# Attention heads of a two-layer trunk: weights issued one head ahead, a second pair of raw buffers, scratch moved between pools, later steps of a head called earlier

## The chip, the cores and the metric

One core of a Trainium2 chip runs the whole program. The time is device microseconds from start to end of one launch; a median over several runs is compared. TensorE (PE) does the matmuls, VectorE (DVE) and ScalarE (ACT) the element work, SyncE (SP) issues nearly all DMAs, and the engines synchronise by semaphores.

## The reference

```python
def reference(x, ...):                       # x: 1 x 1024 x 1024, float32
    h = x
    for layer in range(2):
        u = rmsnorm(h, norm_mix[layer])
        mix = hgrn2_mixer(u, ...) if layer == 0 else dilated_attention_mixer(u, ...)
        h = h + mix
        h = h + swiglu_ffn(rmsnorm(h, norm_ffn[layer]), ...)
    return rmsnorm(h, final_norm)

def dilated_attention_mixer(u, w_qkv, w_out, cos, sin):
    qkv = (u @ w_qkv).reshape(B, S, 3, 12, 128)
    q, k, v = rope(qkv[:, :, 0]), rope(qkv[:, :, 1]), qkv[:, :, 2]
    for gi, (window, dilation) in enumerate(((128, 1), (512, 4), (2048, 16))):   # 4 heads each
        o_g, lse_g = dilated_window_group(q, k, v of the group's heads, window, dilation)
    alpha = softmax over the 3 groups of lse
    return (o * alpha).reshape(B, S, 1536) @ w_out
```

The change lies in the attention mixer of layer 1 alone. The recurrent mixer, both feed-forward layers and the norms stay as they are.

## The kernel before

Everything is float32; a product is made of three single-pass matmuls of a rounded high part and a low part (`halves`: ACT rounds, DVE subtracts). The kernel runs on the Tile framework. The Python text gives each instruction a place in a priority order; when the program is built, a planner with its own estimate of durations fixes the order of each engine's instructions and gives each tile one of the buffers of its tag (`slots`, line 49: "wr" 2, "wx" 2, "wh" 3, "wl" 3, "ws" 4, "va" 16, "vb" 12, "vc" 8, each 128 x 1024 float32). An instruction can be put ahead of earlier text if its inputs and a buffer are there. On the chip each engine then works through its own list strictly in order.

After the values of all heads are made and stored to DRAM (`vd`), the loop over `heads` (line 942) goes through twelve heads in the order (j, gi), head number n = gi * 4 + j, so n = 0, 4, 8, 1, 5, 9, 2, 6, 10, 3, 7, 11. For each head:

- `attn_qk` (line 779) loads the raw weights of q and k (`r_aq`, `r_ak`, 512 KB each, both in "wr"), and `pair` turns them into seven split weights a to g (`pair_weights`, lines 691 to 704, alternating between "wh" and "wl"). Seven products of twelve 512-column matmuls follow (`seeded`, lines 710 to 712): b11, t1, t2, b21, t3, b22, t4, which use the weights a, b, c, d, e, f, g. After every product comes one `tick()`. The partial sums are copied between PSUM banks by ACT (lines 731, 734, 737). `rope` (lines 765 to 777) writes q and k ("vc"), with a scratch tile `sz` ("wx").
- The later steps of a head are put in a calendar by tick: scores in two parts (`s1`, `s2`, lines 829 and 830, with the softmax of line 840 in `s2`), the transposes of the probabilities (`t1`, `t2`, lines 873 and 874) and the product with the values (`values`, lines 883 to 889, with the value tile `avv` in "vc" loaded by `attn_value`). They run in the ticks of the next two heads. The probabilities `ap` lie in "ws": two tiles for a head of group 0 or 1, one for group 2.
- In the group-2 head of j, `attn_merge(j - 1)` (lines 929 to 938) rescales the three outputs of j - 1: six pieces `mg` in "ws", each loaded from `od`, with its weights `dw`, multiplied by DVE (line 937) and stored back.

After the loop the nine merged outputs are loaded (`am`, "vc") and split (`aov0` to `aov8`). `part_out` multiplies them for the first two output blocks d0 and d1 while the last heads' steps still tick. The last three outputs (`late`) are rescaled by `wb`, a broadcast of `dw` that needs all scores of j = 3 (lines 980 to 985), then split as `aov9` to `aov11` and multiplied. `mixer_out` goes on with the other six blocks.

Of the kernel before, what the change touches and what calls it, by code (L numbers as in the profile page):

```python
# [17 lines left out]
D = 1024  # L18
KT = D // P
H = 8  # L20
NH = 12
# [19 lines left out]
def trunk_kernel(ctx, tc, x, cols, consts, w_in, w_hout, w_qkv, w_aout, w_ffn, w_down, out):  # L41
# [9 lines left out]
    def big(tag, name, dt=F32):  # L51
        return gp.tile([P, T], dt, tag=tag, name=name, bufs=slots[tag])
# [4 lines left out]
    def mmps(name):  # L57
        return pmm.tile([P, 512], F32, tag="mm", name=name)
# [4 lines left out]
    def hs(hh):  # L63
        return slice(hh * 512, hh * 512 + 512)

    def cs(c):
        return slice(c * P, c * P + P)


    def load_raw(src, n, name, tag="wr"):  # L70
        raw = big(tag, f"r_{name}")
        nc.sync.dma_start(raw[:, 0:n], src)
        return raw
# [144 lines left out]
    for i0 in range(0, NMASK, 8):  # L218
        n = min(8, NMASK - i0)
# [34 lines left out]
    def hgrn_fq(j):  # L254
        f = scaled(unit(w_in[H + j], v, f"f{j}"), "vc", f"f{j}")
        nc.scalar.activation(f[:], f[:], AF.Sigmoid)
        nc.vector.tensor_scalar(f[:], f[:], omlb[:, j:j + 1], lb[:, j:j + 1], ALU.mult, ALU.add)
        kk = big("vc", f"kk{j}")
        nc.vector.tensor_scalar(kk[:], f[:], -1.0, 1.0, ALU.mult, ALU.add)
        return f, kk, gated(j, 0, "q")  # L260
# [160 lines left out]
    for j in range(H):  # L421
        f, kk, q = hgrn_fq(j)
# [151 lines left out]
    def mixer_out(l, spill, load, vs, parts, name, begun={}):  # L574
        nrm = Norm(name)
        h, ops = {}, {}

        def weights(d):
            n = len(vs) // parts * P
            return [load_w((w_hout, w_aout)[l][d][:, i * n:i * n + n], n, f"{name}w{d}_{i}") for i in range(parts)]  # L580

        for d in DORDER:
            t = big("vc", f"{name}h{d}")
            nc.sync.dma_start(t[:], load[d])
            ws = () if d in begun else weights(d)
            if d == KT - 1:
                w_head[l] = ffn_w_head(l, 0)
            ps = begun.get(d) or [mmps(f"p_{name}{d}_{hh}") for hh in range(2)]
            m = len(vs) // parts
            for i, (whi, wlo) in enumerate(ws):  # L590
                mm3(ps, whi, wlo, 0, vs[i * m:i * m + m], first=(i == 0), last=(i == parts - 1))
            h[d] = add_res(ps, t, d, nrm, spill, 2 * l + 1, name)
            if d >= 4:
                ops[d - 4] = ffn_operands(d - 4, h[d - 4], h[d], op_tags[l][7 * (d - 4):7 * (d - 3)], name)
        return ops, nrm

    ops, nm = mixer_out(0, hd[0], x, ov, 1, "n1")
# [5 lines left out]
    qops = [{n: big("va", f"q{n}_{kk}", F32R) for n in ("b12", "b11")} for kk in range(4)]  # L603
# [83 lines left out]
    def w_half(src, name):  # L687
        wn[0] += 1
        return halves(big(("wh", "wl")[wn[0] % 2], name, F32R), src)

    def pair_weights(ga, up, name):
        g0, g1, u0, u1 = ga[:, hs(0)], ga[:, hs(1)], up[:, hs(0)], up[:, hs(1)]
        w = {"b11": w_half(g0, f"{name}a")}
        nc.vector.tensor_sub(g0, g0, u0)
        nc.vector.tensor_add(u0, u0, u1)
        w["t1"] = w_half(u0, f"{name}b")
        nc.vector.tensor_sub(u0, u1, g0)
        w["t2"] = w_half(u0, f"{name}c")
        w["b21"] = w_half(g1, f"{name}d")
        nc.vector.tensor_sub(g1, g1, u0)  # L700
        w["t3"] = w_half(g0, f"{name}e")
        w["b22"] = w_half(g1, f"{name}f")
        w["t4"] = w_half(u1, f"{name}g")
        return w

    def seeded(ps, w, ops, n, onto=True):
        for kk in range(4):
            wh, wl = w[n][:, cs(kk)], w[n][:, 512 + kk * P:512 + kk * P + P]
            bh, bl = ops[kk][n][:, 0:512], ops[kk][n][:, 512:T]
            nc.tensor.matmul(ps[:], wh, bh, start=(kk == 0 and not onto), stop=False, skip_group_check=onto)  # L710
            nc.tensor.matmul(ps[:], wh, bl, start=False, stop=False, skip_group_check=onto)
            nc.tensor.matmul(ps[:], wl, bh, start=False, stop=(kk == 3), skip_group_check=onto)
# [4 lines left out]
    def later(n, step):  # L717
        steps.setdefault(n, []).append(step)

    def tick():  # L720
        for step in steps.pop(clock[0], ()):
            step()
        clock[0] += 1

    def pair(ga, up, ops, s5, name):
        w = pair_weights(ga, up, name)
        p1, p5, p2, p3 = [mmps(f"{n}_{name}") for n in ("p1", "p5", "p2", "p3")]
        seeded(p1, w, ops, "b11", False)  # L730
        nc.scalar.copy(p2[:], p1[:])
        tick()
        seeded(p5, w, ops, "t1", False)
        nc.scalar.copy(s5, p5[:])
        tick()
        seeded(p2, w, ops, "t2")
        nc.scalar.copy(p3[:], p2[:])
        tick()
        seeded(p1, w, ops, "b21")
        yield p1  # L740
        tick()
        seeded(p3, w, ops, "t3")
        yield p3
        tick()
        seeded(p2, w, ops, "b22")
        yield p2
        tick()
        seeded(p3, w, ops, "t4")
        yield p3
        tick()  # L750
# [25 lines left out]
            nc.vector.tensor_mul(tv, src[:], cb[:, hs(hh)])  # L776
        nc.vector.tensor_add(tv, tv, z)

    def attn_qk(j, gi):
        n = gi * 4 + j  # L780
        ga = load_raw(w_qkv[n], D, f"aq{n}")
        up = load_raw(w_qkv[NH + n], D, f"ak{n}")
        sz = big("wx", f"sz{n}")
        s5, z = sz[:, 0:512], sz[:, 512:T]
        p = pair(ga, up, qops, s5, f"a{n}")
        q = big("vc", f"aq{n}")
        k = big("vc", f"ak{n}")
        rope(q, next(p), None, 0, z)
        rope(k, next(p), s5, 1, z)
        rope(q, next(p), s5, 1, z)  # L790
        rope(k, next(p), None, 0, z)
        for _ in p:
            pass
        return q, k
# [49 lines left out]
    def attn_value(j, gi):  # L844
        n = gi * 4 + j
        vv = big("vc", f"avv{n}")
        src = vd[:, cs(n)]
        if gi == 0:
            nc.sync.dma_start(vv.rearrange("p (c m) -> p c m", m=P), src.rearrange("(c p) m -> p c m", p=P))
        elif gi == 1:  # L850
            sv = src.rearrange("(i p r) m -> p r i m", p=P, r=4)
            for r in range(4):
                nc.sync.dma_start(vv[:, r * 256:r * 256 + 256].rearrange("p (i m) -> p i m", m=P), sv[:, r])
        else:
            nc.sync.dma_start(vv.rearrange("p (c m) -> p c m", m=P), src.rearrange("(p c) m -> p c m", c=8))
        return vv
# [71 lines left out]
    heads = [(j, gi) for j in range(4) for gi in range(3)]  # L928
# [10 lines left out]

    dws = {}  # L940
    sts = [sp.tile([P, 3, 8, 2], F32, tag="st", name=f"st{j}", bufs=2) for j in range(4)]
    for i, (j, gi) in enumerate(heads):
        q, k = attn_qk(j, gi)
        if gi == 2 and j:
            attn_merge(j - 1)
        blocks, ptiles, s1, s2 = attn_scores(j, gi, sts[j], q, k)
        t1, t2, values = attn_out(j, gi, blocks, ptiles)
        vv = {}
        at = clock[0]
        later(at + 2, s1)  # L950
        later(at + 4, s2)
        if gi == 2:
            later(at + 4, lambda j=j: dws.setdefault(j, attn_weights(j, sts[j])))
        later(at + 9, lambda t1=t1, vv=vv, j=j, gi=gi: (vv.setdefault(0, attn_value(j, gi)), t1()))
        later(at + 11, t2)
        later(at + 13, lambda values=values, vv=vv: values(vv[0]))


    ov, begun, aw = [], {}, {}
# [5 lines left out]
    def part_out(d, lo, hi):  # L965
        if d not in begun:
            begun[d] = [mmps(f"p_n3{d}_{hh}") for hh in range(2)]
        i = lo // 6
        if (d, i) not in aw:
            aw[d, i] = load_w(w_aout[d][:, i * 768:i * 768 + 768], 768, f"n3w{d}_{i}")  # L970
        mm3(begun[d], *aw[d, i], (lo - 6 * i) * P, ov[lo:hi], first=(lo == 0), last=(hi == NH))

    d0, d1 = DORDER[:2]
    at = clock[0]
    for upto, d, lo, hi in ((2, d0, 0, 6), (4, d1, 0, 6), (9, d0, 6, 9), (11, d1, 6, 9), (13, None, 0, 0)):
        while clock[0] <= at + upto:
            tick()
        if d is not None:
            part_out(d, lo, hi)
    for gi in range(3):  # L980
        o = late[gi]
        wb = big("wx", f"wb{gi}")
        nc.sync.dma_start(wb[:], dws[3][gi].partition_broadcast(P))
        nc.vector.tensor_mul(o[:], o[:], wb[:])
        ov.append(split(o, "vb", f"aov{9 + gi}"))
# [3 lines left out]
    ops, nm = mixer_out(1, hd[2], hd[1], ov, 2, "n3", begun)  # L989
# [115 lines left out]
```

## Time and profile before

| | |
|---|---|
| median of 3 runs | 2633.09 us (2630.01 to 2633.51) |
| the profiled execution | 2631.86 us, span 2630.1 us |
| TensorE busy | 2538.7 us, 97% of the span |
| VectorE, ScalarE busy | 1739.6 us (66%), 908.0 us (35%) |
| mean granted TensorE clock | 0.987 |

A row of a timeline is start, duration, engine, line, operation, output and inputs, count, and in brackets the idle time of the engine before it with what ended it. A granted clock of 1.00 is TensorE's full 2.4 GHz; 0.5 would be 1.2 GHz throughout.

### The profile page before, as it was taken

How to read it: one execution, taken by the hardware profiler on the slowest of the kernel's cores; microseconds unless marked ns; L12 is line 12 of the kernel's file. 1: busy time of each engine (PE TensorE's matmuls, PEld its weight loads, DVE VectorE, ACT ScalarE, POOL GpSimd, SP SyncE). 2: the span in 40 equal slices, each digit the busy share in tenths (PEclk: the TensorE clock that was granted, in tenths of full speed). 3: DMA queues.
4: the chain of work that ended last, by engine and by line, in shares of the span. 5: the costliest groups of instructions: out<-in, count | busy, mean ns of one | idle time of the engine just before them, and what ended most of it. 6: DMA issues, size and time to landing. Idle time of an engine off the chain costs nothing.

```text
span 2630.1 us, 30557 instructions
## 1 busy us (share of the span) xinstructions
PE 2538.7 (97%) x11804; PEld 2110.8 (80%) x11804; DVE 1739.6 (66%) x3079; ACT 908.0 (35%) x1400; POOL 129.9 (5%) x107
## 2 busy tenths in 40 slices
PE   8999999999999999999999998896999999999998
PEld 6888888778888888888887776775878888887887
DVE  7888888967777776524515665564468777775336
ACT  5222222344232333313423554454343332332212
POOL 1111111111000000000000000000010000000000
PEclk9999999999999999999999998998999999999999
DMA  3111111132222225422232124427422222236323
GB/s 143 33 33 33 33 33 33 49 137 88 88 80 88 80 83 192 159 75 77 81 113 80 49 66 137 135 75 219 137 77 92 85 80 87 74 103 234 107 59 127
DMA packets 113761, 246.78 MB, mean 94 GB/s; under 512 B 23632, under 2 KB 50640, under 8 KB 113616
## 3 DMA queue, kind: packets, MB, share of 16 engines
q1 hardware_dynamic: 113616, 244.83, 28.9%
q8 instruction: 93, 1.52, 0.2%
q14 instruction: 52, 0.43, 0.0%
HBM read 189.07 MB, written 55.72 MB: 93 GB/s over the span
## 4 chain that ended last, share of the span: by engine, by line
PE 77%; DVE 9%; DMA 7%; ACT 4%; issue 2%; POOL 1%; SPq 0%; DVEq 0%; POOLq 0%; ACTq 0%
PE pt L483 6%; PE pt L482 6%; PE pt L481 6%; PE pfw L125 6%; PE pfw L127 6%; PE pfw L124 6%; PE pb L482 4%; PE pb L483 4%; PE pb L481 4%; PE p_n L124 2%; PE p_n L125 2%; PE p_n L127 2%; PE pv L654 2%; PE pv L655 2%; PE pv L656 2%
## 5 line engine op out<-in xcount | busy, mean ns | idle before, releaser
L563 DVE TENSOR_TENSOR h<-pfw,h 128x512 f32<-128x512 f32 (+1 forms) x104 | 63.6, 645 | 197.5 <-PE pfw L127 197.4
L108 ACT CAST h_fw<-r_fw 128x896 fp32r<-128x896 f32 (+1 forms) x60 | 58.2, 973 | 237.6 <-PE pfw L125 216.9
L108 ACT CAST h_fa<-r_fg 128x1024 fp32r<-128x1024 f32 x44 | 46.5, 1056 | 199.7 <-PE pt L482 184.8
L108 ACT CAST h_fb<-s 128x1024 fp32r<-128x1024 f32 x44 | 46.4, 1054 | 171.2 <-PE pb L482 159.6
L829 PE MATMUL as<-ak,aq 128*128 128x256 f32 (+1 forms) x192 | 64.6, 455 | 30.2 <-DVE st L830 22.9
L342 DVE COPY_PREDICATED at<-lm,lv 128x192 f32<-128x192 uint8 (+2 forms) x288 | 82.0, 352 | 4.2 <-PE lv L327 3.3
L829 PEld LDWEIGHTS as<-ak,aq 128*128 128x128 f32 x192 | 46.5, 281 | 42.2 <-DVE st L830 28.1
L156 POOL TENSOR_TENSOR rs_n<-ms_n,half 128x8 f32<-128x8 f32 (+2 forms) x7 | 9.3, 1334 | 1359.0 <-DVE ms_n L154 1359.0
L655 PE MATMUL pv<-vw,qb 128*128 128x512 f32 x192 | 74.8, 390 | 0.0
L654 PE MATMUL pv<-vw,qb 128*128 128x512 f32 x192 | 74.8, 389 | 0.0
L656 PE MATMUL pv<-vw,qb 128*128 128x512 f32 x192 | 74.7, 389 | 0.0
L494 DVE TENSOR_TENSOR s<-r_fu 128x512 f32<-128x512 f32 x44 | 30.3, 691 | 63.5 <-DMA r_fu<-in_w_ffn_dram 63.5
L482 PE MATMUL pb<-n3b,h_fa 128*128 128x512 f32 x176 | 68.7, 390 | 2.6 <-DVE n3b L456 2.6
L109 DVE TENSOR_TENSOR l_fw<-r_fw,h_fw 128x896 fp32r<-128x896 f32 (+1 forms) x60 | 67.0, 1120 | 5.5 <-ACT h_fw L108 4.8
L482 PE MATMUL pb<-n1b,h_fa 128*128 128x512 f32 x176 | 68.6, 390 | 1.2 <-DVE n1b L456 1.2
L481 PE MATMUL pb<-n3b,h_fa 128*128 128x512 f32 x176 | 68.8, 391 | 0.5 <-ACT n3b L455 0.5
L481 PE MATMUL pt<-n3t,h_fb 128*128 128x512 f32 x176 | 68.9, 392 | 0.0
L483 PE MATMUL pt<-n3t,l_fb 128*128 128x512 f32 x176 | 68.7, 390 | 0.0
L482 PE MATMUL pt<-n3t,h_fb 128*128 128x512 f32 x176 | 68.7, 390 | 0.0
L481 PE MATMUL pb<-n1b,h_fa 128*128 128x512 f32 x176 | 68.6, 390 | 0.0
L481 PE MATMUL pt<-n1t,h_fb 128*128 128x512 f32 x176 | 68.6, 390 | 0.0
L483 PE MATMUL pb<-n3b,l_fa 128*128 128x512 f32 x176 | 68.5, 389 | 0.0
(1505 smaller groups left out, 7949.1 us busy)
## 6 DMA issues: line engine op xcount, KB each, us to landing
r_fu<-in_w_ffn_dram SPq DMA_DIRECT2D x44, 512.0 KB, 3.6
r_fg<-in_w_ffn_dram SPq DMA_DIRECT2D x44, 512.0 KB, 3.6
act<-g SPq DMA_DIRECT2D x44, 512.0 KB, 2.6
st<-act SPq DMA_DIRECT2D x44, 512.0 KB, 4.2
r_fw<-in_w_down_dram SPq DMA_DIRECT2D x44, 448.0 KB, 3.4
h<-hd SPq DMA_DIRECT2D x16, 512.0 KB, 5.6
r_fw<-in_w_down_dram SPq DMA_DIRECT2D x16, 512.0 KB, 3.6
vr<-in_w_qkv_dram SPq DMA_DIRECT2D x24, 256.0 KB, 3.2
```

The source lines that it names most:

```text
L108: nc.scalar.copy(hi[:, a:b], src[:, a:b])
L124: nc.tensor.matmul(p[:, 0:b - a], wh, vh[:, a:b], start=(first and i == 0), stop=False)
L125: nc.tensor.matmul(p[:, 0:b - a], wh, vl[:, a:b], start=False, stop=False)
L127: nc.tensor.matmul(p[:, 0:b - a], wl, vh[:, a:b], start=False, stop=(last and i == n - 1))
L342: nc.vector.copy_predicated(av[:, :, d:4, :], mk[:, :, d:4, :], pv[:, :, s0:s0 + 4 - d, :])
L481: nc.tensor.matmul(ps[:], wh, bh, start=(kk == 0), stop=False)
L482: nc.tensor.matmul(ps[:], wh, bl, start=False, stop=False)
L483: nc.tensor.matmul(ps[:], wl, bh, start=False, stop=(kk == 3))
L654: nc.tensor.matmul(ps[:], vh, wh, start=(kb == 0), stop=False)
L655: nc.tensor.matmul(ps[:], vh, wl, start=False, stop=False)
L656: nc.tensor.matmul(ps[:], vl, wh, start=False, stop=(kb == 7))
L829: nc.tensor.matmul(ps[:, o:o + w], tok(q, gi, b * P, P), tok(k, gi, ks[0] * P, w), start=True, stop=True)
```

## The change

A new `qk_weights` issues the loads and the splitting of a head's weights; the loop calls it one head ahead. The raw k weights go to "wx", so that two heads' raw weights can be in memory at once; the scratch `sz` moves from "wx" to "vc". In the calendar `t1` moves from 9 to 8 ticks after the head, `t2` from 11 to 9, `values` from 13 to 10. After the loop the parts of the output product are cut and placed differently between the ticks, and `wb` moves from "wx" to "wr".

```diff
-    def pair(ga, up, ops, s5, name):
-        w = pair_weights(ga, up, name)
+    def pair(w, ops, s5, name):
...
-    def attn_qk(j, gi):
+    def qk_weights(j, gi):
         n = gi * 4 + j
         ga = load_raw(w_qkv[n], D, f"aq{n}")
-        up = load_raw(w_qkv[NH + n], D, f"ak{n}")
-        sz = big("wx", f"sz{n}")
+        up = load_raw(w_qkv[NH + n], D, f"ak{n}", "wx")
+        return pair_weights(ga, up, f"a{n}")
+
+    def attn_qk(j, gi, w):
+        n = gi * 4 + j
+        sz = big("vc", f"sz{n}")
...
+    qw = {heads[0]: qk_weights(*heads[0])}
     for i, (j, gi) in enumerate(heads):
-        q, k = attn_qk(j, gi)
+        if i + 1 < NH:
+            qw[heads[i + 1]] = qk_weights(*heads[i + 1])
+        q, k = attn_qk(j, gi, qw.pop((j, gi)))
...
-        later(at + 9, lambda ...: (vv.setdefault(0, attn_value(j, gi)), t1()))
-        later(at + 11, t2)
-        later(at + 13, lambda ...: values(vv[0]))
+        later(at + 8, lambda ...: (vv.setdefault(0, attn_value(j, gi)), t1()))
+        later(at + 9, t2)
+        later(at + 10, lambda ...: values(vv[0]))
...
-    for upto, d, lo, hi in ((2, d0, 0, 6), (4, d1, 0, 6), (9, d0, 6, 9), (11, d1, 6, 9), (13, None, 0, 0)):
+    for upto, d, lo, hi in ((1, d0, 0, 3), (4, d0, 3, 6), (4, d0, 6, 9), (9, d1, 0, 6), (10, d1, 6, 9)):
         while clock[0] <= at + upto:
             tick()
-        if d is not None:
-            part_out(d, lo, hi)
+        part_out(d, lo, hi)
     for gi in range(3):
         o = late[gi]
-        wb = big("wx", f"wb{gi}")
+        wb = big("wr", f"wb{gi}")
```

## Rows read from the trace of the kernel before

**Rows 1.** The page, part 1: busy time, share of the span, instructions

```profile
PE 2538.7 (97%) x11804; PEld 2110.8 (80%) x11804; DVE 1739.6 (66%) x3079; ACT 908.0 (35%) x1400; POOL 129.9 (5%) x107
```

**Rows 2.** Stretches: bounds, length, busy PE PEld DVE ACT POOL, clock, DMA share, GB/s

```profile
1576.60:1614.00 37.40, 30.01 (x140) 25.61 (x138) 19.08 (x42) 13.79 (x25) 0.00 (x0) 0.86 0.65 183
1775.70:1846.10 70.40, 50.49 (x220) 40.17 (x219) 32.55 (x55) 29.18 (x48) 0.00 (x0) 0.85 0.70 213
1846.10:1944.50 98.40, 98.40 (x436) 81.50 (x435) 46.83 (x63) 34.04 (x51) 8.30 (x6) 1.00 0.34 111
```

**Rows 3.** Waits of TensorE in the loop over heads: total, times, longest

```profile
PE as L829 <- DVE st L830: 22.9, 9, 5.6
...
PE p_a L710 <- ACT p_a L731: 4.6, 3, 2.5
```

**Rows 4.** A wait of TensorE from the loop's end to 1850 us

```profile
PE p_n L124 <- ACT aov0h L144: 4.3, 1, 4.3
```

**Rows 5.** Timeline at head 5, DVE, SP and PE, weights of head 9

```profile
1522.04 0.68 DVE L612 TENSOR_TENSOR a5g<-r_ak,a5g 128x512 fp32r<-128x512 f32 x1
1522.75 0.33 SPq L72 DMA_DIRECT2D r_ak<-in_w_qkv_dram  x1
1526.52 0.69 DVE L694 TENSOR_TENSOR r_aq<-r_aq,r_ak 128x512 f32<-128x512 f32 x1 [1.79 <-DMA r_ak<-in_w_qkv_dram]
1527.86 0.42 DVE L830 CUSTOM_DVE_ANT_0 ap<-as,kon 128x256 f32<-128x256 f32 x1
1528.34 1.13 PE L829 MATMUL as<-ak,aq 128*128 128x256 f32 x4 [2.09 <-DVE st L830]
```

**Rows 6.** Stretches after such waits, columns as in rows 2

```profile
1495.60:1504.60 9.00, 7.17 (x27) 6.06 (x27) 5.25 (x20) 1.72 (x3) 0.00 (x0) 0.81 0.02 9
...
1658.00:1678.50 20.50, 19.43 (x93) 16.68 (x94) 11.91 (x32) 9.82 (x27) 0.00 (x0) 0.92 0.01 1
1750.00:1760.00 10.00, 9.18 (x26) 6.77 (x27) 4.67 (x13) 3.57 (x7) 0.00 (x0) 0.83 0.44 124
```

**Rows 7.** Timeline at the start of head 11, ACT and PE

```profile
1744.79 2.18 ACT L889 COPY ao<-apo 128x512 f32<-128x512 f32 x2
1750.19 0.58 ACT L731 COPY p_a<-p_a 128x512 f32<-128x512 f32 x1
1750.82 0.50 PE L710 MATMUL p_a<-qt,a11c 128*128 128x512 f32 x1 [2.47 <-ACT p_a L731]
```

**Rows 8.** Timeline at the end of the merges, DVE and PE

```profile
1607.31 0.68 DVE L937 TENSOR_TENSOR mg<-mg 128x512 f32<-128x512 f32 x1
1608.26 0.84 PE L829 MATMUL as<-ak,aq 128*128 128x128 f32 x2 [5.58 <-DVE st L830]
1708.56 0.84 PE L829 MATMUL as<-ak,aq 128*128 128x128 f32 x2 [4.95 <-DVE st L830]
```

**Rows 9.** Timeline of the loop's end, PE, SP and DVE

```profile
1772.35 3.51 PE L883 MATMUL apo<-ap,avv 128*128 128x128 f32 x30
1774.55 0.47 SPq L935 DMA_DIRECT2D mg<-od  x1
1806.27 0.28 DVE L830 CUSTOM_DVE_ANT_0 ap<-as,even 128x128 f32<-128x128 f32 x1
1818.76 0.52 SPq L905 DMA_DIRECT2D dn<-st  x1
1835.98 1.65 PE L124 MATMUL p_n<-aov9h,h_n3w 128*128 128x512 f32 x3 [10.23 <-ACT aov9h L144]
```

**Rows 10.** Instructions of line 710: durations in ns, first and last start

```profile
L710 PE MATMUL p_a<-qt,a0b x4: 389/389/389, 1410.7 to 1412.7; 128*128 128x512 f32 x4
...
L710 PE MATMUL p_a<-qt,a0e x4: 389/389/389, 1418.8 to 1420.9; 128*128 128x512 f32 x4
```

**Rows 11.** DMA issues, 1400 to 1850 us: count, KB each, median us to landing

```profile
r_ak<-in_w_qkv_dram SPq DMA_DIRECT2D x11, 512.0 KB, 5.0
avv<-vd SPq DMA_DIRECT2D x8, 512.0 KB, 6.1
```

More of the change, by code (lines that the diff above doesn't have):

```diff
@@ L777, in rope @@
         nc.vector.tensor_add(tv, tv, z)
-    def attn_qk(j, gi):
+    def qk_weights(j, gi):
         n = gi * 4 + j
         ga = load_raw(w_qkv[n], D, f"aq{n}")
-        up = load_raw(w_qkv[NH + n], D, f"ak{n}")
-        sz = big("wx", f"sz{n}")
+        up = load_raw(w_qkv[NH + n], D, f"ak{n}", "wx")
[3 more added lines that the diff above has]
+        sz = big("vc", f"sz{n}")
         s5, z = sz[:, 0:512], sz[:, 512:T]
-        p = pair(ga, up, qops, s5, f"a{n}")
+        p = pair(w, qops, s5, f"a{n}")
         q = big("vc", f"aq{n}")
@@ L953, in trunk_kernel @@
             later(at + 4, lambda j=j: dws.setdefault(j, attn_weights(j, sts[j])))
-        later(at + 9, lambda t1=t1, vv=vv, j=j, gi=gi: (vv.setdefault(0, attn_value(j, gi)), t1()))
-        later(at + 11, t2)
-        later(at + 13, lambda values=values, vv=vv: values(vv[0]))
+        later(at + 8, lambda t1=t1, vv=vv, j=j, gi=gi: (vv.setdefault(0, attn_value(j, gi)), t1()))
+        later(at + 9, t2)
+        later(at + 10, lambda values=values, vv=vv: values(vv[0]))
     ov, begun, aw = [], {}, {}
```

## The prediction

> **What bounds the kernel now.** I read the page first: TensorE is busy for 97% of the span [rows 1], so only work or idle time of TensorE can move the end. The busy share by stretch comes next. Behind the attention mixer TensorE has no idle time at all: 98.4 us busy of 98.4, at full clock [rows 2]. What is saved before that point is therefore kept. Inside the mixer it is different: one head that holds a merge takes 37.4 us with 30.0 busy at a clock of 0.86, and the end of the mixer 70.4 us with 50.5 busy at 0.85 [rows 2]. The third view is what TensorE waits for. In the loop over heads 22.9 us go to nine waits of the score matmuls (line 829) for the DVE instruction that empties the scores' bank (line 830), and 4.6 us to three waits for an ACT copy between banks (line 731) [rows 3]. At the end there are waits of 4.3 us for the first merged output [rows 4] and 10.23 us for `aov9`, the first of the last three [rows 9]. The timelines say why.
>
> Two of the nine waits, 5.58 and 4.95 us, come right behind the last merge multiplication on DVE [rows 8]; they are the merges' and I keep them apart. The other seven add up to 22.9 - 10.5 = 12.4 us. Rows 5 show one of 2.09 us. DVE makes the seventh weight of head 5 out of `r_ak`; only then is a "wr" buffer free, 0.7 us later SP issues the next head's `r_ak`, and DVE sits until 1526.52 on line 694, which needs it. The score eviction is queued behind lines 694 and 695, and TensorE behind the eviction [rows 5]. So one pair of raw buffers makes each head's weights late, and DVE's list carries the lateness to TensorE. The clock drops after such waits: in the 9.0 us from 1495.6 it is 0.81, in the 20.5 us from 1658 it is 0.92 [rows 6], which is (1 - 0.81) x 9.0 = 1.7 and (1 - 0.92) x 20.5 = 1.6 us of lost full-speed time. I count four such drops behind the seven waits.
>
> **The change part by part.** No matmul, element operation or byte is added: the products, the splits and the DMAs are the same, and cutting a part of the output product in two keeps its matmuls. Everything is a question of when.
>
> *Raw weights a head ahead, in two pairs.* The load of head i + 1 no longer waits for the seventh weight of head i; it needs the buffers that head i - 1 left, a head or seven products earlier, against 5.0 us from issue to landing [rows 11]. The split weights still wait for "wh" and "wl" (six buffers for seven weights), so a of head i + 1 can be written when product b of head i is done. That is one product ahead of the scores, which tick after the third; one product takes (1418.8 - 1410.7) / 3 = 2.7 us [rows 10], and DVE needs about three operations of 0.69 us [rows 5] in it. Lines 694 and 695 then stand in front of the scores without a DMA to wait for. Worth 12.4 + 4 x 1.7 = 19.2 us. Bounds: 0, if the planner puts still more of the next head's splitting in front of the evictions, since it now has the better priority; and 19.2. I take 19.2, as the row names the DMA as the releaser.
>
> *`values` three ticks sooner.* The copies of a head's output out of PSUM (line 889, 2.18 us) now fall in the middle of a head. In head 11 they stood on ACT, at the head's start, in front of the copy of line 731 for which TensorE waited 2.47 us [rows 7]. This wait should go, with the slow clock after it, (1 - 0.83) x 10.0 = 1.7 us [rows 6]: 4.2 us. The other two of its kind are 4.6 - 2.5 = 2.1 us together [rows 3]; I leave them as they are. Worth 4.2, bounds 0 (if the copies hold up another bank copy where they now stand) and 6.3.
>
> *The same step at the loop's end.* `values` of head 9 frees the "ws" buffers of its probabilities, and the last merge starts on them: its first load goes out 2.2 us after these matmuls start, at 1774.55. It runs through two buffers until the scores of head 11 at last get a "ws" buffer, at 1806.27, and from their end hangs the chain to `wb` and `aov9` [rows 9]. Three products sooner is 3 x 2.7 = 8.1 us: merge, scores, `wb` and `aov9` all move by it. The value buffer freed with it also lets the first merged output be loaded sooner, so the 4.3 us wait [rows 4] goes too, inside the same 8.1. Worth 8.1. The upper bound is 19.9, TensorE's whole idle time there, 70.4 - 50.5 [rows 2]; it needs the scores and softmax, which now take 1818.76 - 1806.27 = 12.5 us [rows 9] among output matmuls, to go undisturbed, as the new places of `part_out` allow. The lower is 0: `wb` now shares the two "wr" buffers with the output weights, and if it gets only one of them its three loads go one after the other.
>
> *The merges inside the loop.* They also start 8.1 us sooner against TensorE's list. But the planner placed the scores by its own idea of when a merge ends, and will do so again; the chip's DMAs were later than that by the 5.58 and 4.95 us, and will be again. I take 0. Bounds: a gain of the two waits and of the slow clock of the merge heads, 10.5 + (1 - 0.86) x 37.4 = 15.7 us [rows 8, 2]; a loss of as much as the waits, 10.5, if DVE, which now meets merge pieces in mid-head, holds up weights there.
>
> *`sz` in "vc".* This is the part that costs. "vc" has eight buffers. `cb` and `sb` hold two for the whole loop; while product five of a head ends, q and k of two heads hold four, `sz` one and the output of the head before one. That is eight of eight, with none left for the next value tile, which takes 6.1 us to land [rows 11]; it can come only when the older q and k are done. Before, `sz` was not among them. A wait for a "vc" buffer is not in this trace; I bound it by nothing and by one wait like the 2.09 us one [rows 5] with its 1.7 us of slow clock in each of eleven heads, 42 us. I take 5, nearer to nothing, because `values` three ticks sooner gives back the value tile 8.1 us sooner and so pays for most of the extra buffer.
>
> *At nothing:* the first head's `r_ak` now waits for a "wx" buffer of the v stage, while the products of the values' last tokens still run on TensorE; product a does not need it. If that cover is too short, product b is late by about the 5.0 us of the load [rows 11], once.
>
> The sum, against the profiled execution's own 2631.86 us (span 2630.1 and 1.8 around it): 2631.86 - 19.2 - 4.2 - 8.1 + 5 = 2605.4. The median of the runs is 1.2 us above that execution, so I say 2606.
>
> **The rivals.**
>
> *The merges' waits go too.* If the planner gives head 5's and head 8's scores buffers freed by `values` of the head before, which now runs near the scores, the wait becomes one on TensorE's own work. For it: that step is three ticks nearer. Against: the merge pieces come first in priority. 2606 - 15.7 = 2590.
>
> *The raw weights were not the limit.* The wait is for DVE, and DVE's own work in front of line 830 may be enough to hold it: the planner hands the next head's splitting a better priority than the evictions. For it: lines 694 and 695 take 1.3 us of the 2.09 in rows 5 in any case. Against: the 1.79 us on the DMA in the same rows. Then only the other parts stay: 2631.86 - 4.2 - 8.1 + 5 = 2624.6, and 1.2 for the median, 2626.
>
> *Slower: "vc" is short.* One mechanism: the second rope tile of a head finds no buffer until the scores of the head before are done, TensorE's seventh product waits for its bank, and so does every head. Price 3.8 us a head, 42 in all: 2606 - 5 + 42 = 2643. It decides from 31.5 / 11 = 2.9 us a head on (31.5 is the sum of the gains). For it: eight of eight above. Against: the scores that free q and k tick in that very product. The Trainium skill speaks for this rival (Perfetto Trace Analysis, Optimization Strategy): a gap that repeats along a stretch, on the engine that should be saturated, can mean that there is no room for the next tile. The seven waits of rows 3 agree with it, as what was short there was a raw buffer; by that rule the change cures one shortage and makes another in "vc", and the time would be that of this rival.
>
> *No change to speak of:* a bubble of 2.9 us a head eats the gain: 2633.
>
> **How the numbers follow.** The forecast, with what lies between 2595 and 2615, has 0.52; the merges gone too 0.16; raw weights not the limit 0.14; no change 0.08; slower 0.10. What a measurement of this kernel can tell from no change is about 0.2%, 5.3 us. So faster 0.82, same 0.08, slower 0.10. The range leaves out the slower cases and most of no change, and a little below the merges' case: 2582 to 2630.
>
> **What would show it.** Right: no DMA as releaser in front of line 694; the waits of line 829 for line 830 down from nine to the merges' two and few small ones; line 731 no more behind line 889; `values` of head 9 ahead of the last three products of head 11; the last merge some 8 us sooner against the loop's end, and the wait for `aov9` shorter than 10.2 us. Wrong: waits of ACT or DVE on a "vc" buffer in every head, with TensorE behind them, or line 830 just as late behind line 612 without any DMA. The prediction fails if the planner's new order puts TensorE behind something that this trace does not show.

## The result, and the profile after

The changed kernel takes 2607.75 us (median of four runs, 2606.18 to 2614.0) against 2631.55 us before: a ratio of 0.9914 with a 95% interval of 0.9895 to 0.9933. The profiled execution is the one of 2606.18 us, with a span of 2604.4. The forecast, 2606, was met. Its sum was not: two of its terms are wrong by 14 to 19 us each, with opposite signs, and the experiments show which.

First the page's part 1 of the changed kernel (answers to rows 1):

```profile
PE 2537.0 (97%) x11804; PEld 2103.8 (81%) x11804; DVE 1741.9 (67%) x3079; ACT 910.3 (35%) x1400; POOL 129.9 (5%) x107
```

Its stretches, with the columns of rows 2, are the head with the first merge, the time from the loop's end (the last product with weight g of head 11) to the end of the idle time, and the same 98.4 us of full work as before:

```profile
1574.35:1606.80 32.45, 29.61 (x137) 24.60 (x136) 21.92 (x49) 18.51 (x48) 0.00 (x0) 0.95 0.56 179
1759.10:1818.00 58.90, 48.89 (x208) 37.42 (x209) 30.44 (x53) 29.44 (x58) 0.00 (x0) 0.88 0.69 207
1818.00:1916.40 98.40, 98.40 (x436) 81.48 (x435) 46.57 (x62) 36.38 (x53) 8.31 (x6) 1.00 0.35 113
```

The work is the same and TensorE's last stretch too; what is gone is idle time and slow clock. The first merge's head takes 32.45 us instead of 37.40 [rows 2], at a clock of 0.95 instead of 0.86. From the loop's first matmul (line 710, at 1407.82, now 1408.85) to the first one behind the output product (1944.48, now 1918.81) the time falls from 536.7 to 510.0 us. Cut where both the loop's last matmul and the product of head 9 are done (1775.7, now 1759.1), the loop gives 367.9 - 350.3 = 17.6 of it and the end 168.8 - 159.7 = 9.1. Next, TensorE's waits in the loop, then those from 1750 to 1850 us (total, times, longest):

```profile
PE as L832 <- DVE st L833: 6.2, 4, 2.2
PE apo L886 <- DMA avv<-vd: 5.1, 3, 2.3
PE as L832 <- DVE ak L776: 3.1, 6, 1.1
...
PE p_a L710 <- ACT p_a L730: 0.8, 1, 0.8
...
PE p_n L124 <- ACT aov9h L144: 7.4, 1, 7.4
```

Lines 832 and 833 were 829 and 830: their 22.9 us in nine waits are 6.2 in four, and the copy (line 730, was 731) has 0.8 instead of 4.6 us [rows 3]. A new row stands second: the product waits for a load of the values, `avv`. The end's wait is 7.4 instead of 10.23 us [rows 9]. The instructions of line 694, first in the kernel before, then in the changed one, where they have no DMA among their releasers any more:

```profile
L694 DVE TENSOR_TENSOR r_aq<-r_aq,r_ak x12: 682/692/693, 1406.1 to 1731.3; 128x512 f32<-128x512 f32 x12
...
  DMA r_ak<-in_w_qkv_dram: 6.2, 6
```

```profile
L694 DVE TENSOR_TENSOR r_aq<-r_aq,r_ak x12: 686/687/692, 1407.2 to 1710.9; 128x512 f32<-128x512 f32 x12
...
its engine sat idle before it (us, times) until:
who waited for it (us, times):
```

The merges changed most. The timelines of SP and DVE show the first inner merge, beginning with the kernel before (its end is in rows 8):

```profile
1575.23 0.54 SPq L901 DMA_DIRECT2D dn<-st  x1
1575.86 0.58 SPq L935 DMA_DIRECT2D mg<-od  x1
1583.94 0.69 DVE L937 TENSOR_TENSOR mg<-mg 128x512 f32<-128x512 f32 x1 [4.50 <-DMA mg<-dw]
1593.16 0.69 DVE L937 TENSOR_TENSOR mg<-mg 128x512 f32<-128x512 f32 x1 [4.92 <-DMA mg<-od]
1603.69 0.69 DVE L937 TENSOR_TENSOR mg<-mg 128x512 f32<-128x512 f32 x1 [3.32 <-DMA mg<-dw]
```

and then the changed one, with SP's issues of `avv`'s loads and TensorE behind them:

```profile
1565.48 0.38 SPq L938 DMA_DIRECT2D mg<-od  x1
1574.08 0.69 DVE L940 TENSOR_TENSOR mg<-mg 128x512 f32<-128x512 f32 x1
1582.75 0.69 DVE L940 TENSOR_TENSOR mg<-mg 128x512 f32<-128x512 f32 x1 [0.78 <-DMA mg<-dw]
1585.71 0.32 SPq L941 DMA_DIRECT2D od<-mg  x1
1586.12 0.93 SPq L856 DMA_DIRECT2D avv<-vd  x2
1590.32 0.94 SPq L856 DMA_DIRECT2D avv<-vd  x2
1592.88 0.69 DVE L940 TENSOR_TENSOR mg<-mg 128x512 f32<-128x512 f32 x1 [1.60 <-DMA mg<-dw]
1594.72 2.13 PE L886 MATMUL apo<-ap,avv 128*128 128x128 f32 x12 [2.32 <-DMA avv<-vd]
```

Before, the merge's first load went out 0.7 us ahead of this head's start (1576.60, rows 2); now it goes 8.9 us ahead of it (1574.35). Its first multiplication waited 4.50 us for the load, and now finds it there. Over all three merges DVE's waits for these loads fall from 31.5 to 6.7 us, and the two waits of TensorE behind the merges [rows 8] are gone.

Two waits of some 2 us stay in front of line 832, and they have a new releaser. The DVE and PE timelines at head 6:

```profile
1618.36 0.17 DVE L913 TENSOR_TENSOR amx<-cm 128x8 f32<-128x8 f32 x1 [2.17 <-DMA cm<-dn]
1618.44 0.69 DVE L694 TENSOR_TENSOR r_aq<-r_aq,r_ak 128x512 f32<-128x512 f32 x1
1619.88 0.41 DVE L833 CUSTOM_DVE_ANT_0 ap<-as,kon 128x256 f32<-128x256 f32 x1
1620.36 1.13 PE L832 MATMUL as<-ak,aq 128*128 128x256 f32 x4 [2.06 <-DVE st L833]
```

It is the shape of rows 5 with another load at its head: the statistics' round trip through `cm` instead of `r_ak`.

### The profile page after: what moved, and what is told of

It reads as the page before. It is cut to its first block, busy times and chain, and to the rows that moved or that the text cites. A ratio compares the mean times of both kernels' runs of the same rounds, so it can differ in the third digit from the quotient of the medians.

```text
span 2604.4 us, 30576 instructions
## 1 busy us (share of the span) xinstructions
PE 2537.0 (97%) x11804; PEld 2103.8 (81%) x11804; DVE 1741.9 (67%) x3079; ACT 910.3 (35%) x1400; POOL 129.9 (5%) x107
## 4 chain that ended last, share of the span: by engine, by line
PE 79%; DVE 9%; DMA 5%; ACT 3%; issue 2%; POOL 1%; SPq 0%; DVEq 0%; POOLq 0%; ACTq 0%
PE pt L481 6%; PE pt L482 6%; PE pt L483 6%; PE pfw L125 6%; PE pfw L127 6%; PE pfw L124 6%; PE pb L482 4%; PE pb L483 4%; PE pb L481 4%; PE p_n L125 2%; PE p_n L124 2%; PE p_n L127 2%; PE pv L654 2%; PE pv L655 2%; PE pv L656 2%
## 5 line engine op out<-in xcount | busy, mean ns | idle before, releaser
L108 ACT CAST h_fb<-s 128x1024 fp32r<-128x1024 f32 x44 | 46.4, 1054 | 171.2 <-PE pb L482 159.7
L483 PE MATMUL pb<-n1b,l_fa 128*128 128x512 f32 x176 | 68.5, 389 | 0.0
L483 PE MATMUL pt<-n1t,l_fb 128*128 128x512 f32 x176 | 68.5, 389 | 0.0
```

What stands on the lines that cost most here:

```text
L108: nc.scalar.copy(hi[:, a:b], src[:, a:b])
L483: nc.tensor.matmul(ps[:], wl, bh, start=False, stop=(kk == 3))
```

## The experiments

Times here are ratios to the kernel before on the same chip, with 95% intervals; a price in us is (1 - ratio) x 2632.

**The change taken apart.** *The weights alone*: the diff's hunks on `pair`, `qk_weights`, `attn_qk` and `qw`, with the calendar of `later` and the tail as before.

> Of the change, the weights alone: issued a head ahead, raw k weights in wx, scratch sz in vc; calendar, parts of the output product and wb as before. If the late raw weights were the cost of the seven score waits, no instruction of line 694 waits for the DMA of r_ak any more, and the time is 10 to 18 us under that of before (2613 to 2622), with the two merge waits of about 5 us still there. If the calendar carries the whole gain, the time is that of before within 5 us.

Measured 0.9948 [0.9934, 0.9961], 13.7 us. Line 694 waits for no DMA; TensorE's waits behind the merges shrink to 3.06 and 3.79 us, but they stay.

*The calendar alone*:

```
-        later(at + 9, lambda ...: (vv.setdefault(0, attn_value(j, gi)), t1()))
-        later(at + 11, t2)
-        later(at + 13, lambda ...: values(vv[0]))
+        later(at + 8, ...t1...)
+        later(at + 9, t2)
+        later(at + 10, ...values...)
```

> Of the change, the calendar alone: t1, t2 and values 8, 9 and 10 ticks after the head. If the earlier release of the probabilities' buffers starts the merges sooner and the planner follows, the two merge waits of about 5 us go and the end moves up by about 8 us: 2610 to 2618, with seven waits of 1 to 3 us behind line 694 as before. If the weights carry the whole gain, or if the planner puts the scores as far ahead of the merges as before, the time is 2622 or more, and the merge waits are still there.

Measured 0.9902 [0.9889, 0.9916], 25.8 us: these three lines give as much as the whole change, and more than the 14 to 22 us expected of them. The two merge waits behind line 830 are gone. The seven others did not stay as expected either: TensorE waits 4.6 us in four for line 830, though line 694 still waits 7.9 us in seven for the raw weights. TensorE's waits for line 777 rise, which is taken up below.

*All but the calendar* (the changed kernel with ticks 9, 11 and 13, and 13 for the last part of the output product):

> The changed kernel with the old calendar (9, 11, 13; the last part of the output product waits for tick 13). If the places of the output product's parts bring nothing by themselves, this is the time of the weights alone. If the last scores ahead of most of the output product are worth something without the calendar, it is 5 us or more under the weights alone.

Measured 0.9951 [0.9939, 0.9964], 12.9 us, no other than the weights alone.

*All but the tail* (`part_out` in its old places, `wb` in "wx"):

> The changed kernel with the parts of the output product and wb's buffers as before. If the gain at the end comes from the merge starting three products sooner, the time is that of the changed kernel within 3 us (2604 to 2611) and the wait for aov9 is 7 to 8 us. If it comes from the new places of the parts, the time is 5 to 9 us above the changed kernel and the wait for aov9 is 10 us or more.

Measured 0.9916 [0.9903, 0.993]. The changed kernel, run again in the next set, gave 0.9911 [0.9897, 0.9925]: the tail's places are worth nothing that can be measured. The other half of the expectation failed: the wait for `aov9` is 10.4 us with the old places against 7.4 with the new ones. So that wait got shorter by the new places, and the time did not.

> The changed kernel once more, beside the kernels of this call: 0.990 to 0.993 of before.

*Calendar and tail, weights as before*:

> Calendar and end as in the changed kernel, but the weights as before (one raw pair, not ahead, scratch in wx). If the weights bring nothing once the calendar is moved, this is the changed kernel's time within 5 us, and the wait for aov9 is 7 us or less. If the weights bring what they bring alone, it is 8 us or more above the changed kernel.

Measured 0.9903 [0.9889, 0.9916]. So the weights, worth 13.7 us alone, add nothing to the calendar. DVE still waits for the raw weights in this kernel. Its instructions of line 694, and DVE's timeline at the scores of one head:

```profile
L694 DVE TENSOR_TENSOR r_aq<-r_aq,r_ak x12: 684/692/694, 1408.4 to 1712.9; 128x512 f32<-128x512 f32 x12
its engine sat idle before it (us, times) until:
  DMA r_ak<-in_w_qkv_dram: 6.4, 6
```

```profile
1498.73 0.69 DVE L612 TENSOR_TENSOR a5a<-r_aq,a5a 128x512 fp32r<-128x512 f32 x1 [1.23 <-ACT a5a L611]
1499.34 0.28 DVE L830 CUSTOM_DVE_ANT_0 ap<-as,even 128x128 f32<-128x128 f32 x1
...
1499.55 0.28 DVE L830 CUSTOM_DVE_ANT_0 ap<-as,even 128x128 f32<-128x128 f32 x1
...
1499.76 0.69 DVE L694 TENSOR_TENSOR r_aq<-r_aq,r_ak 128x512 f32<-128x512 f32 x1
```

Here the score evictions come ahead of line 694; in the kernel before, lines 694 and 695 stood between a5a and them. The raw weights are as late, but TensorE is mostly no longer queued behind them: its waits for line 830 are 3.8 us in four. Another row has grown, though; the kernel before had 5.2 us in five there, the calendar alone has 11.5 in six, the changed kernel 3.1 in six:

```profile
PE as L829 <- DVE ak L777: 12.3, 7, 3.8
```

```profile
1588.10 0.69 DVE L937 TENSOR_TENSOR mg<-mg 128x512 f32<-128x512 f32 x1 [2.96 <-DMA mg<-dw]
1592.04 1.32 PE L829 MATMUL as<-ak,aq 128*128 128x128 f32 x4 [3.80 <-DVE ak L777]
```

Line 777 ends the rope of k. In the two heads with an inner merge it stands in DVE's list behind a merge multiplication that waited for its load, and TensorE waits 3.80 and 3.01 us for it: with the old weights the merges still hold TensorE, through another line. The changed kernel has no such wait in these heads, but its products wait for `avv` in the loop, and its time is no better.

**Which part of the calendar.** *Only the statistics and the preparation (ticks 8 and 9), `values` left at 13*:

> The kernel before with t1 and t2 8 and 9 ticks after the head, values still at 13. If it is values that counts (the probabilities' buffers given to the merge, the output copies off the head's start), the time is that of before within 5 us and the merge waits of about 5 us stay. If the transposes and their copies count, it is 8 us or more faster.

Measured 0.9951 [0.9939, 0.9964], 12.9 us, so the transposes count; but the merges' waits of 4.99 and 4.84 us stay. The other 12.9 us come with `values` at 10, and with them these two waits go (those of line 777 come, as shown above). With `values` at 13 the first merge's first load still goes out only 1.0 us ahead of the head, as SP's and TensorE's timelines show:

```profile
1577.27 0.33 SPq L935 DMA_DIRECT2D mg<-od  x1
1578.29 0.48 PE L710 MATMUL p_a<-qb,a2a 128*128 128x512 f32 x1
```

Yet DVE's waits for the loads of the three merges fall from 31.5 to 13.9 us (3.9 more have no releaser in the profile). So half of the calendar's gain comes without an earlier first load of this merge.

**Buffers or place in the text.** *The weights called a head ahead, but one raw pair in "wr", and `sz` in "wx"*:

> The kernel before with the weights called one head ahead in the text, but still one pair of raw buffers in wr and the scratch in wx. If the buffers made the weights late, line 694 still waits for the DMA of r_ak in most heads and the time is that of before within 5 us. If the place in the text counts, it is that of the weights alone, 10 to 14 us faster.

Measured 1.0015 [1.0005, 1.0024]: the call's place alone gives nothing. Line 694 waits 12.1 us in seven for the DMA, and TensorE 5.49 and 6.04 us behind the merges. It takes the second pair of buffers (and `sz` out of "wx", which makes room for it). The Trainium skill (Perfetto Trace Analysis, Optimization Strategy) says that a repeated gap can mean too little room for the next tile; for the raw weights these runs agree.

**The price of `sz` in "vc".** The kernel with calendar and tail, and one line more:

```
-        sz = big("wx", f"sz{n}")
+        sz = big("vc", f"sz{n}")
```

> The new calendar and the new tail, weights as before, and the swapped copies in the value buffers (vc) instead of the weight buffers (wx). It prices that one move. Mine: the price of the prediction, 0 to 5 us over the run with calendar and tail alone (ratio 0.990 to 0.9925). Rival of the prediction: the value buffers are short; 10 us or more over it (ratio 0.994 or above).

Measured 0.99 [0.9886, 0.9913]: no price at all.

**Are the merges what the calendar cures?** *The kernel before without the three inner merges*:

```
-        if gi == 2 and j:
-            attn_merge(j - 1)
```

> The kernel before without the three inner merges of the mixer's loop (the rescaling of nine heads' outputs is left out; the last merge stays). If the loop's gain under the new calendar comes through the merges, which hold VectorE and the score buffers while they wait, this one is already 15 to 25 us faster than the kernel before (ratio 0.990 to 0.994). If the gain comes from where the calendar puts TensorE's and ScalarE's work, leaving the merges out is worth no more than their two waits of 5 us (ratio 0.996 or above).

> The same as the run without inner merges, with the new calendar (statistics at 8, output preparation at 9, product at 10) added. If the calendar's gain works through the merges, this stands within 6 us of the run without merges. Rival: the calendar's gain is its own; then it is 12 to 20 us under the run without merges.

Measured 0.9875 [0.9862, 0.9889] without merges, more than the 15 to 25 us expected, and 0.9874 [0.9859, 0.9889] without merges and with the calendar. The calendar, worth 25.8 us with the merges, is worth nothing without them. The merges' price, their own work included, was 32.9 us in the kernel before; with the calendar alone it is about (0.9902 - 0.9874) x 2632 = 7.4, in the changed kernel (0.9914 - 0.9874) x 2632 = 10.5. The waits of TensorE without merges, first with the old calendar, then with the new one:

```profile
PE as L829 <- DVE st L830: 18.2, 9, 2.8
PE as L829 <- DVE ak L777: 3.1, 5, 1.3
...
PE p_a L710 <- ACT p_a L731: 1.7, 2, 1.0
```

```profile
PE p_a L710 <- ACT p_a L731: 11.0, 3, 4.3
PE as L829 <- DVE ak L777: 4.6, 5, 1.3
PE as L829 <- DVE st L830: 3.8, 5, 1.8
```

The calendar takes 14.4 us from the evictions' waits here too, and 9.3 us come back in front of line 710. With the cut used above, behind head 9's product with the values, the loop takes 353.5 and 351.6 us and the end 152.6 and 155.6: what the loop gains the end loses. A releaser that loses its row has not given its time back. The same cut shows where the merges' price lay: in the kernel before 367.9 - 353.5 = 14.4 us in the loop and 168.8 - 152.6 = 16.2 at the end; with the calendar alone (351.3 and 161.5) nothing in the loop and 161.5 - 155.6 = 5.9 at the end. These are single profiled executions from different sets, so a few us of this are no finding.

**A try at the new wait.** The six loads and stores of each merge issued from POOL, so that `avv`'s loads don't stand behind them on SP:

```
-                nc.sync.dma_start(oh, o[:, hs(hh)])
+                nc.gpsimd.dma_start(oh, o[:, hs(hh)])
 (and so for wb and the store)
```

> The changed kernel with the six loads and stores of each merge issued from POOL instead of SP; nothing else differs. Theory: in the changed kernel two products (apo) wait 2.3 us each for a load of avv, because that load stands on SP behind the merge's loads and stores, which wait for VectorE there. Then these waits are gone, SP issues avv's loads at once, and the time is 4 to 10 us under the changed kernel (a ratio to the kernel before of 0.987 to 0.990). Rival: the wait is avv's own transfer, or POOL's issues start later and lengthen the merge; then the ratio stays at 0.991 or rises, up to 0.996 if the last merge comes later.

Measured 0.9975 [0.9966, 0.9984], 16 us slower than the changed kernel. The first half of the theory holds: SP issues the four loads of `avv` from 1583.02 us on, and the product waits for none. But the merge got worse. POOL's, DVE's and TensorE's timelines:

```profile
1566.58 0.75 POOL L938 DMA_DIRECT2D mg<-od  x1 [278.61 <-DVE aq L772]
1577.99 1.22 POOL L941 DMA_DIRECT2D od<-mg  x2 [9.02 <-DVE ng L841]
1580.78 0.55 POOL L938 DMA_DIRECT2D mg<-od  x1 [1.58 <-issue]
1582.45 0.55 POOL L939 DMA_DIRECT2D mg<-dw  x1
1589.65 0.69 DVE L940 TENSOR_TENSOR mg<-mg 128x512 f32<-128x512 f32 x1 [4.75 <-DMA mg<-dw]
1600.15 0.69 DVE L940 TENSOR_TENSOR mg<-mg 128x512 f32<-128x512 f32 x1 [4.06 <-DMA mg<-dw]
1602.94 0.84 PE L832 MATMUL as<-ak,aq 128*128 128x128 f32 x2 [3.79 <-DVE st L833]
```

The merge starts early here too: its first load goes out 10.7 us ahead of the head (1577.28). But the second pair's loads follow it only after 14.2 us (11.6 from SP), and their multiplication comes 8.9 us after the first of them (5.6 from SP); DVE waits 4 us and more again, 22.2 us for `mg<-dw` over all three merges (6.7 from SP), and TensorE waits 3.79 and 3.91 us behind the merges, as it did before the change.

## Why the prediction was right, and where it was not

*Raw weights a head ahead, 19.2 us: the mechanism is right for about half of the waits, its worth in this sum is wrong.* The load was late for want of a buffer, and DVE's order carried it to TensorE: line 694's DMA wait is gone and the second pair does it. But line 694 waited only 6.2 us for that DMA in all, against the 12.4 us of TensorE's seven waits that I put down to it; the wait of 1.83 us behind a5a (at 1498.72 us) had no DMA in front of it, only lines 694 and 695 themselves. With the weights alone, 12.7 - 3.06 - 3.79 = 5.9 us of such waits stay. Alone the part is worth 13.7 us, inside my bounds of 0 to 19.2. But the prediction added it to the rest "as the row names the DMA as the releaser". With the calendar most evictions stand ahead of line 694 in DVE's list, so the lateness has little behind it (read from the timelines, no run tests it), and the part is worth nothing more. The rival "the raw weights were not the limit" had the right worth for this part, in part for another reason, and missed the total because it kept my zero for the merges.

*The merges inside the loop, 0: this is the step that failed.* I wrote that the planner "placed the scores by its own idea of when a merge ends, and will do so again". However it did, the loads now go out 8.9 instead of 0.7 us ahead of the head, and DVE waits 6.7 instead of 31.5 us for them. With the merges left out the calendar is worth nothing; with them it takes their price from 32.9 to 7.4 us. The merges' price in the loop, 14.4 us, lies beside the upper bound I gave for this step, 15.7, and that is the value I should have taken. The rival "the merges' waits go too" was right that they go; that the scores got buffers freed by `values` was not traced. Its 2590 was not reached, since it kept the 19.2 us as well.

*`values` sooner, 4.2 us, and the loop's end, 8.1 us: the places are right, the sizes in part by chance.* TensorE waits 0.8 us for line 730 where it waited 4.6 for line 731. The calendar by itself did not give this: with it alone the wait in head 11 is gone, but one of 3.4 us stands in front of the same copy in head 5. The last merge's first load is issued at 1747.65 instead of 1774.55 us, 11.5 us ahead of the loop's last matmul at 1759.1 (before, 2.2 us behind its last, at 1772.35). That is 13.7 us sooner where I had 8.1: I took a tick for a product's 2.7 us, but TensorE's other work and waits lie between the products, and a seventh of a head was 367.9 / 84 = 4.4 us. The end is 9.1 us shorter where I had 8.1. What follows in the changed kernel (answers to rows 9):

```profile
1747.65 0.33 SPq L938 DMA_DIRECT2D mg<-od  x1
1794.27 0.51 SPq L908 DMA_DIRECT2D dn<-st  x1
1810.57 1.65 PE L124 MATMUL p_n<-aov9h,h_n3w 128*128 128x512 f32 x3 [7.41 <-ACT aov9h L144]
```

The gain comes from the calendar: the new places of `part_out` are worth nothing measurable, and `wb` in "wr" costs nothing.

*`sz` in "vc", 5 us:* nothing. With it falls the slower rival and its rule; no run shows a price of it. What did appear was a wait for `avv`'s load, which SP issues between the merge's loads and stores; the prediction did not look at SP's queue.

So 2606 (the sum gives 2605.4 + 1.2 = 2606.6) was met by luck, with wrong parts: 19.2 us for something that the calendar makes worthless, 0 for what carries the gain, 5 for a cost that isn't there. That the calendar works through the merges is shown. Left open is which of their resources it relieves first. It moves their loads' issue, frees the "ws" buffers they share with the probabilities, and moves DVE's list; runs without merges take away all three at once, and no run gave "ws" another buffer. An early first load is not enough and not all of it: half of the gain came with a lead of 1.0 us, and from POOL a lead of 10.7 us did not keep the gain. Nor was it tried whether the second raw pair is worth something once the merges are gone.

## What to carry to other kernels

Two waits that end on the same engine's in-order list are not two gains: price each cure alone and on top of the other before adding them. When a wait stands behind a staged load, look at how far ahead of its use each of its pieces is issued, not the first alone, and what holds them back; three due times gave here what new buffers and a new tail did not add to. And a row of waits that disappears is no gain until the stretch is shorter.

## What the runs showed of the hardware

DMAs issued from POOL cost more than from SP here: 0.55 us on the issuing engine for each load of a merge against medians of 0.37 and 0.42 on SP, and a median of 4.6 us to landing against 4.1, at most 8.7 against 6.4. The Trainium skill (DMA: Bandwidth & Descriptors, SWDGE vs HWDGE vs iDMA) says that POOL's descriptors are computed by software and set up more slowly than SP's; the trace agrees. How much of the 16 us is this, and how much the loads that stand behind stores in POOL's one list, was not separated.

Two profiled executions of the changed kernel, from two sets of runs, differ by 10.5 us (2606.18 and 2616.69) and by 9.3 us in the mixer alone (510.0 and 519.3), while the ratios to the kernel before in the same set are 0.9914 and 0.9911. A difference of a few us between traces of two sets is no finding; the ratios are.
